# Differential attention: the rotary rows of a query or key tile are gathered by DMA and turned once a head

## The chip, the core and the metric

One core of a Trainium2 chip runs the whole program: two transformer blocks of two layers each, in one launch. The metric is the device time of one execution in microseconds. Three runs of the kernel before took 2494.85, 2496.67 and 2498.16 us; the median is 2496.67. The core has TensorE (matrix products and transposes through the identity), VectorE, ScalarE, GpSimd, and SyncE, which here only issues DMAs.

## The reference, cut to what matters

Sequence 512, model width 1024. The second layer of the first block is a differential attention with 8 heads. A head has two queries and two keys of 64 numbers and one value of 128. Of each 64 numbers only the first 16 are rotated by position, in pairs of number i and number i + 8:

```
q = _partial_rope(q, positions, 16, 500000.0)   # x1*cos - x2*sin , x2*cos + x1*sin on the first 16
k = _partial_rope(k, positions, 16, 500000.0)   # the other 48 of 64 pass unchanged
p1 = softmax(causal(q1 @ k1.T * 64 ** -0.5)); p2 = softmax(causal(q2 @ k2.T * 64 ** -0.5))
o = (p1 - lam * p2) @ v
o = rmsnorm(o, subln) * (1 - lambda_init)       # per head, then the output projection
```

The order of the 64 numbers within q and k may be changed in both alike, since only their dot products are used.

## The kernel before, in words

All products are taken in float32 quality as three float32r matmuls: an operand is split into a high part (a cast on ScalarE) and a low part (a subtraction, mostly on VectorE), by `split` (line 310), and `mm3` (line 345) adds high x high, high x low and low x high. Weights come in tiles of 128x1024 through SyncE: `dma_next` (line 134) loads one into one of two `raw` buffers, `split_next` (line 153) splits it into one of five `whi`/`wlo` pairs, and the next load waits until a `raw` buffer is free again.

The stage `diff` (line 970) holds everything of the attention. Activations lie transposed, numbers in partitions, 512 positions in columns. `fhead` (line 365) makes the query and key tiles of heads 0 and 1, half the columns at a time, while the layer norm before it finishes. `v_half` (line 958) makes the values in two halves. `projs(h)` (line 1027) is a generator which makes the query and then the key tile of a head, 24 matmuls each, in steps of 3. It gives control back after every step, and it waits at its gate until `self.unit`, the count of query tiles scored, is high enough. Every finished tile goes to `evac` (line 1004).

`evac` rotates all 128 rows by `rope` (line 652): a shuffle of the partitions out of PSUM on VectorE, a product with the cosine table, a product of the shuffled tile with the signed sine table, and an addition on GpSimd. The tables have 1 and 0 for rows that aren't rotated. Then it splits: a query's high part by a ScalarE cast, its low part on GpSimd, for each of the two halves of 64 rows; a key's high part twice by ScalarE casts and its low part on VectorE. After that `ready` holds the tile.

`attend` (line 623) walks over 8 heads and 4 query tiles. For a tile it emits `scores` (line 1034, eight matmuls in two PSUM banks, two softmaxes without normalising, and line 1054, which joins the two probability tiles), puts off the transposes of the joined tile by 6500 (`put`, key `sm`), and then lets `fill` (line 389) run a budget of other work from the queue `fq`, here the value half, the projections of heads 2 to 7, and the output projection. The budgets stand in `PLAN`: 30 for each of the first four tiles, then 11, and 9 for the last head. After a head's fourth tile come the value product `o`, sums of squares, and the scaling (`post`, line 1059).

Work that is put off stands in a list with due times (`defer`, line 321). The clock of that list counts TensorE columns as they are emitted (`tick`, line 328), and `need` (line 336) empties the list until something is ready. This gives the order of the program text. In `diff` only GpSimd keeps that order by hand (`hand=("Pool",)`). On TensorE, VectorE, ScalarE and SyncE a scheduler orders the instructions from its own estimate of when each is ready, earlier text first.

Of the kernel before, what the change touches and what calls it, by code (L numbers as in the profile page):

```python
# [9 lines left out]
F32 = mybir.dt.float32  # L10
F32R = mybir.dt.float32r
I32 = mybir.dt.int32
AF = mybir.ActivationFunctionType
ALU = mybir.AluOpType
# [3 lines left out]
D = 1024  # L18
S = 512
# [3 lines left out]
LAMBDA_INIT = 0.8 - 0.6 * math.exp(-0.3)  # L23
DFF1, DFF2 = 4096, 2816
MLA_SWAP = [i ^ 16 for i in range(32)]
DIFF_SWAP = [i ^ 8 if i < 16 else i for i in range(32)]
RING = 5
RAW = 2
AUTO = True
# [1 line left out]

PLAN = {
    "mla": dict(hand=("SP", "Pool"), ln=7000, sm=6000, pv=2500, eb=3, gate=5, cq=1500, n=([5] * 4 + [6] * 4) * 3 + [5] * 4 + [9] * 4),
    "diff": dict(hand=("Pool",), qp=1, kp=0, vp=1, wp=0, rp=0, nb=2, ln=7000, rot=3500, sm=6500, pv=2500, eb=3, sums=1000, scale=5500, n=[30] * 4 + [11] * 24 + [9] * 4),
    "fox": dict(ln=5500, sm=4200, pv=1500, eb=2, n=[30] * 4 + [11] * 24 + [9] * 4),
    "ret": dict(ln=5500, y=3900, n=30),
    "f0": dict(ln=7000), "f1": dict(ln=8500), "g0": dict(ln=5500), "g1": dict(ln=5500),
# [3 lines left out]
class Net:  # L41
# [620 lines left out]

    def rope_tables(self, pool, tmp, which, tags=("t0", "t1", "t2"), bufs=1):
        nc = self.nc
        C = pool.tile([128, S], F32, name="ropeC", bufs=1)
        Sn = pool.tile([128, S], F32, name="ropeS", bufs=1)
        pi = tmp.tile([128, S], I32, tag=tags[0], name="pi", bufs=bufs)
        a = tmp.tile([128, S], F32, tag=tags[1], name="ang", bufs=bufs)
        k = tmp.tile([128, S], F32, tag=tags[2], name="kk", bufs=bufs)
        inv = self.col[:, 2 * which:2 * which + 1]  # L670
        sgn = self.col[:, 2 * which + 1:2 * which + 2]
        (nc.gpsimd if which else nc.sync).dma_start(out=pi, in_=self.A["positions"].to_broadcast([128, S]))
        nc.vector.tensor_copy(a, pi)
        nc.vector.tensor_scalar(a, a, inv, None, op0=ALU.mult)
        MAG = 12582912.0
        nc.vector.tensor_scalar(k, a, 1.0 / (2 * math.pi), MAG, op0=ALU.mult, op1=ALU.add)
        nc.vector.tensor_scalar(k, k, -MAG, None, op0=ALU.add)
        c1 = 6.28125
        c2 = float(np.float32(2 * math.pi - c1).view(np.int32) & -4096)
        c2 = float(np.int32(np.float32(2 * math.pi - c1).view(np.int32) & -4096).view(np.float32))  # L680
        c3 = float(np.float32(2 * math.pi - c1 - c2))
        for cc in (c1, c2, c3):
            nc.vector.scalar_tensor_tensor(a, k, -cc, a, op0=ALU.mult, op1=ALU.add)
        PIF = 3.1415925
        nc.vector.tensor_scalar(a, a, PIF, -PIF, op0=ALU.min, op1=ALU.max)
        nc.scalar.activation(Sn, a, AF.Sin)
        nc.vector.scalar_tensor_tensor(a, a, -1.0, a, op0=ALU.mult, op1=ALU.min)
        nc.vector.tensor_scalar(a, a, math.pi / 2, None, op0=ALU.add)
        nc.scalar.activation(C, a, AF.Sin)
        nc.vector.tensor_scalar(Sn, Sn, sgn, None, op0=ALU.mult)  # L690
        return C, Sn

    def setup(self):
# [276 lines left out]
    def diff(self):  # L970
        nc, A, tc = self.nc, self.A, self.tc
        mm = nc.tensor.matmul
        with ExitStack() as outer:
# [27 lines left out]
            kls = [kz[:, 2 * i:2 * i + 2, :] for i in range(2)]  # L1001
            places = self.whole("c", F32)

            def evac(h, which):
                def f(ps):
                    r = self.rope(p, ps, DIFF_SWAP, C, Sn)


                    if which == 0:
                        qk[h] = [self.rs(n, F32R).rearrange("p (a n) -> p a n", a=2) for n in ("qa", "ka")]  # L1010
                        qk[h].append(kls[h % 2])
                    q, k, kl = qk[h]
                    for i in range(2):
                        own, other = slice(64 * i, 64 * i + 64), slice(64 - 64 * i, 128 - 64 * i)
                        if which == 0:
                            self.split(q[own, i, :], q[other, i, :], r[own], eng=nc.gpsimd if self.plan["qp"] else None)
                        else:
                            self.split(k[own, i, :], kl[own, i, :], r[own], eng=nc.gpsimd if self.plan["kp"] else None)
                            nc.scalar.copy(k[other, i, :], r[own])
                    ready.add((h, which))  # L1020
                return f

            self.fhead(4, lambda i, ps: evac(i // 2, i % 2)(ps))
            for _ in self.v_half(VH, VL, 0):
                pass

            def projs(h):
                for i in range(2):
                    while self.unit < 4 * h - 4 - (i == 0):
                        yield 0  # L1030
                    yield from self.proj(self.get, 0, 8, self.XH, self.XL, evac(h, i))
                self.need(lambda: (h, 1) in ready)

            def scores(h, qt):
                n, ts = qt * 128 + 128, slice(qt * 128, qt * 128 + 128)
# [23 lines left out]
            def post(h, o):  # L1059
                sq = places[:, 3, :]  # L1060
                nc.scalar.activation(sq, o, AF.Square)
                ot = p.tile([128, S], F32, tag="ot", name="ot", bufs=1)
                nc.scalar.copy(ot, o)
                rr = self.small(4, "rr")

                def sums():
                    sps = self.ps("sps")
                    for t in range(NT):
                        mm(sps[:, 2 * t:2 * t + 2], sq[:, t * 128:t * 128 + 128], ones, start=(t == 0), stop=(t == NT - 1))
                        self.tick(128, 4)  # L1070
                    s8 = self.small(8, "s8")
                    nc.vector.tensor_copy(s8, sps[:, 0:8])

                    nc.vector.tensor_tensor(rr, s1[h], s1[h], op=ALU.mult)
                    nc.vector.tensor_scalar(rr, rr, 1e-6, None, op0=ALU.mult)
                    nc.vector.scalar_tensor_tensor(rr, s8.rearrange("p (t a) -> p t a", a=2)[:, :, 0], 1.0 / 128, rr,
                                                   op0=ALU.mult, op1=ALU.add)
                    nc.gpsimd.tensor_tensor(rr, rr, self.mh, op=ALU.pow)
                    self.defer(self.plan["scale"], scale)

                def scale():
                    bp = self.ps("bp")
                    for t in range(NT):
                        self.transpose(bp[:, t * 128:t * 128 + 128], rr[:, t:t + 1].to_broadcast([128, 128]))
                    nc.vector.scalar_tensor_tensor(ot, ot, sub, bp, op0=ALU.mult, op1=ALU.mult)
                    self.split(VH[:, h, :], VL[:, h, :], ot, eng=nc.gpsimd if self.plan["vp"] else None)
                    nready[0] = h + 1

                self.defer(self.plan["sums"], sums)
# [334 lines left out]
ROPE_ORDER = np.array([16 * (i // 32) + i % 16 + 32 * (i % 32 // 16) for i in range(64)])  # L1424


def constants():
    c = {}
    c["c_idn"] = np.eye(128, dtype=np.float32)
    i = np.arange(128)  # L1430
    c["c_mask"] = np.zeros((128, S), np.float32)
    c["c_mask"][:, S - 128:] = np.where(i[None, :] <= i[:, None], 0.0, NEG)
    col = np.zeros((128, 16), np.float32)
    col[:, 0] = (10000.0 ** (-2.0 * (ROPE_ORDER[i % 64] % 32) / 64.0)).astype(np.float32)
    col[:, 1] = np.where(ROPE_ORDER[i % 64] < 32, -1.0, 1.0)
    d = i % 64
    col[:, 2] = np.where(d < 16, 500000.0 ** (-2.0 * (d % 8) / 16.0), 0.0).astype(np.float32)
    col[:, 3] = np.where(d < 8, -1.0, np.where(d < 16, 1.0, 0.0))
    c["c_col"] = col
    rows = np.zeros((32, 16), np.float32)  # L1440
    r = np.arange(32)
    kind = r // 8
    rows[:, 0] = kind == 0
    rows[:, 1] = kind == 1
    rows[:, 2] = kind >= 2
    rows[:, 3] = -1.0 * (kind == 2)
    rows[:, 4] = -1.0 * (kind == 3)
    rows[:, 5] = kind < 2
    rows[r, 8 + r % 8] = 1.0
    c["c_rows"] = rows  # L1450
    inv = (10000.0 ** (-np.arange(128) / 128.0)).astype(np.float32)
    ang = (np.arange(S, dtype=np.float32)[None, :] * inv[:, None]).astype(np.float32).astype(np.float64)
    c["c_rcos"] = np.cos(ang).astype(np.float32)
    c["c_rsin"] = np.sin(ang).astype(np.float32)
    key, q = np.arange(128)[:, None], np.arange(S)[None, :]
    dec = np.zeros((4, 128, S), np.float32)
    for h in range(4):
        gam = 1.0 - 2.0 ** (-5.0 - h)
        dec[h] = np.where(q // 64 >= key // 64, gam ** np.abs(q - key), 0.0)
    c["c_decay"] = dec  # L1460
    return c


def layout(I):
# [23 lines left out]
    for i in range(2):  # L1488
# [9 lines left out]
        n = DFF2 // 128  # L1498
# [3 lines left out]
        A[f"w_in{i}"] = gu.reshape(n // 2, 4, 128, D)[1:]  # L1502
        A[f"w_out{i}"] = pack_h(np.asarray(I["ffn_w_out_2"])[i])

    def heads(w):
        q, k = pack_f(w[:, :D]), pack_f(w[:, D:2 * D])
        v = np.concatenate([pack_v(np.ascontiguousarray(w[:, 2 * D + j * 512:2 * D + j * 512 + 512])) for j in range(2)])
        qk = np.stack([q, k], axis=1).reshape(16, 128, D)
        return np.concatenate([qk[:4], v, qk[4:]])

    A["w_d"] = heads(np.asarray(I["diff_w_qkv"])[0])
    A["w_do"] = pack_h(np.asarray(I["diff_w_o"])[0])
    wx = np.asarray(I["fox_w_in_2"])[0]
    A["w_x"] = heads(wx[:, :3 * D])
# [29 lines left out]
```

## Time and profile before

| | |
|---|---|
| median of the runs shown | 2496.67 us |
| the profiled execution | 2495.72 us |
| its span | 2492.5 us |
| TensorE busy | 2445.1 us (98%) |
| VectorE busy | 1644.9 us (66%) |
| ScalarE busy | 1113.9 us (45%) |
| GpSimd busy | 358.9 us (14%) |

The profile shows one execution. The span is the time from the first to the last instruction on record; the execution takes 3.2 us more. Busy shares are averages over eight stages with different limits. The granted TensorE clock was 0.997 of full speed over the span, which is the level of 2.4 GHz.

### The profile page before, as it was taken

How to read it: one execution, taken by the hardware profiler on the slowest of the kernel's cores; microseconds unless marked ns; L12 is line 12 of the kernel's file. 1: busy time of each engine (PE TensorE's matmuls, PEld its weight loads, DVE VectorE, ACT ScalarE, POOL GpSimd, SP SyncE). 2: the span in 40 equal slices, each digit the busy share in tenths (PEclk: the TensorE clock that was granted, in tenths of full speed). 3: DMA queues.
4: the chain of work that ended last, by engine and by line, in shares of the span. 5: the costliest groups of instructions: out<-in, count | busy, mean ns of one | idle time of the engine just before them, and what ended most of it. 6: DMA issues, size and time to landing. Idle time of an engine off the chain costs nothing.

```text
span 2492.5 us, 35902 instructions
## 1 busy us (share of the span) xinstructions
PE 2445.1 (98%) x14624; PEld 2176.4 (87%) x14624; DVE 1644.9 (66%) x2295; ACT 1113.9 (45%) x1664; POOL 358.9 (14%) x311
## 2 busy tenths in 40 slices
PE   9999999999989999999999999999999999999998
PEld 8889889888778988987888999988888888999987
DVE  6978758666987755755655877744454555877743
ACT  5635535424663543544454544533322233444532
POOL 2103002012342301104000222100000000222100
PEclk9999999999999999999999999999999999999999
DMA  4312332323121233232222333232322223233232
GB/s 151 109 68 94 97 126 87 102 79 102 52 90 61 88 103 129 82 102 87 85 68 77 102 102 104 90 100 83 124 79 86 81 85 107 81 118 111 77 104 73
DMA packets 65860, 233.40 MB, mean 94 GB/s; under 512 B 7536, under 2 KB 7680, under 8 KB 65696
## 3 DMA queue, kind: packets, MB, share of 16 engines
q1 hardware_dynamic: 62064, 219.21, 26.9%
q0 software_dynamic: 3488, 11.55, 1.4%
q8 instruction: 114, 1.87, 0.3%
q10 hardware_dynamic: 144, 0.36, 0.1%
q14 instruction: 50, 0.41, 0.1%
HBM read 228.99 MB, written 2.10 MB: 93 GB/s over the span
## 4 chain that ended last, share of the span: by engine, by line
PE 52%; POOL 1%; DVE 0%; ACT 0%; issue 0%; DVEq 0%; POOLq 0%; ACTq 0%
PE zA L266 3%; PE zA L267 3%; PE zA L268 3%; PE ta L349 2%; PE ta L347 2%; PE ta L348 2%; PE tb L349 2%; PE tb L348 2%; PE tb L347 2%; PE ps L347 2%; PE ps L349 2%; PE ps L348 2%; PE pj L347 2%; PE pj L349 2%; PE pj L348 2%; PE v L347 2%
## 5 line engine op out<-in xcount | busy, mean ns | idle before, releaser
L313 ACT CAST whi<-raw 128x1024 fp32r<-128x1024 f32 (+3 forms) x347 | 359.5, 1038 | 592.3 <-PE ta L349 143.0
L314 DVE TENSOR_TENSOR wlo<-raw,whi 128x1024 fp32r<-128x1024 f32 (+3 forms) x347 | 430.3, 1243 | 281.8 <-ACT whi L313 281.5
L314 DVE TENSOR_TENSOR wlo<-qt,whi 128x1024 fp32r<-128x1024 f32 x102 | 168.0, 1647 | 33.5 <-ACT whi L313 33.5
L347 PE MATMUL ps<-XH,whi 128*128 128x256 f32 (+1 forms) x576 | 177.9, 309 | 0.0
L348 PE MATMUL ps<-XL,whi 128*128 128x256 f32 (+1 forms) x576 | 176.7, 307 | 0.0
L349 PE MATMUL ps<-XH,wlo 128*128 128x256 f32 (+1 forms) x576 | 176.7, 307 | 0.0
L267 PE MATMUL zB<-XL,whi 128*128 128x256 f32 x544 | 154.1, 283 | 0.3 <-DVE XL L314 0.3
L268 PE MATMUL zB<-XH,wlo 128*128 128x256 f32 x544 | 153.9, 283 | 0.0
L266 PE MATMUL zB<-XH,whi 128*128 128x256 f32 x544 | 153.9, 283 | 0.0
L313 ACT CAST whi<-qt 128x1024 fp32r<-128x1024 f32 x102 | 107.1, 1050 | 96.8 <-PE zA L267 75.8
L196 POOL TENSOR_TENSOR qt<-raw,qt 128x1024 f32<-128x1024 f32 x34 | 98.1, 2885 | 307.4 <-DVE wlo L314 251.0
L196 POOL TENSOR_TENSOR qt<-qr,raw 128x1024 f32<-128x1024 f32 x34 | 85.4, 2512 | 339.7 <-PE ta L348 182.3
L347 PE MATMUL pj<-XH,whi 128*128 128x512 f32 x288 | 116.7, 405 | 0.0
L349 PEld LDWEIGHTS ps<-XH,wlo 128*128 128x128 f32 x576 | 109.8, 191 | 5.1
L348 PEld LDWEIGHTS ps<-XL,whi 128*128 128x128 f32 x576 | 109.9, 191 | 5.0
L347 PEld LDWEIGHTS ps<-XH,whi 128*128 128x128 f32 x576 | 109.9, 191 | 5.0
L349 PE MATMUL pj<-XH,wlo 128*128 128x512 f32 x288 | 113.0, 392 | 0.0
L348 PE MATMUL pj<-XL,whi 128*128 128x512 f32 x288 | 112.5, 390 | 0.0
L267 PEld LDWEIGHTS zB<-XL,whi 128*128 128x128 f32 x544 | 104.4, 192 | 0.5 <-DVE XL L314 0.5
L314 DVE TENSOR_TENSOR wlo<-qr,whi 128x1024 fp32r<-128x1024 f32 x68 | 83.3, 1226 | 31.9 <-ACT whi L313 31.8
L268 PEld LDWEIGHTS zB<-XH,wlo 128*128 128x128 f32 x544 | 104.4, 192 | 0.0
L266 PEld LDWEIGHTS zB<-XH,whi 128*128 128x128 f32 x544 | 104.4, 192 | 0.0
(480 smaller groups left out, 7462.9 us busy)
## 6 DMA issues: line engine op xcount, KB each, us to landing
raw<-in_w_r SPq DMA_DIRECT2D x48, 512.0 KB, 3.5
raw<-in_w_out SPq DMA_DIRECT2D x44, 512.0 KB, 3.4
qr<-in_w_in SPq DMA_DIRECT2D x40, 512.0 KB, 4.4
raw<-in_w_in SPq DMA_DIRECT2D x40, 512.0 KB, 3.5
raw<-in_w_d SPq DMA_DIRECT2D x24, 512.0 KB, 3.5
raw<-in_w_x SPq DMA_DIRECT2D x24, 512.0 KB, 3.4
raw<-in_w_dn0a SPq DMA_DIRECT2D x16, 512.0 KB, 3.5
raw<-in_w_dn0b SPq DMA_DIRECT2D x16, 512.0 KB, 3.4
```

The costliest lines, as they stand in the source:

```text
L196: eng.tensor_tensor(t, a, b, op=ALU.subtract)
L266: mm(out, a, sh[:, k, :], start=f, stop=False, skip_group_check=True)
L267: mm(out, a, sl[:, k, :], start=False, stop=False, skip_group_check=True)
L268: mm(out, b, sh[:, k, :], start=False, stop=e, skip_group_check=True)
L313: nc.scalar.copy(hi, src)
L314: (eng or nc.vector).tensor_tensor(lo, src, hi.bitcast(F32), op=ALU.subtract)
L347: mm(ps, ah, bh, start=first, stop=False)
L348: mm(ps, ah, bl, start=False, stop=False)
L349: mm(ps, al, bh, start=False, stop=last)
```

## The change

Query and key weights are packed with a new order of columns (`DIFF_ORDER`), so that the rotated numbers of both halves of a tile lie in rows 48 to 79, the two of a pair side by side. A finished tile is copied whole out of PSUM to `rq` by ScalarE. Three DMAs on SyncE's queue gather its 32 rows: straight into `rot`, and with the two of each pair exchanged into rows 64 and up of `swp`. When both tiles of a head are there, `turn` does three VectorE operations on 64 rows and two DMAs put the rows back into `rq`. `parts` does the splits that `evac` did before, and only it makes the head `ready`. `turn` is put off by 3000 after the key tile's copy, `parts` by another 5000. At the head of the stage, the tiles of head 1 are held in PSUM until `parts(0)` has run.

The tables share one tile, cosine in rows 0 to 63, signed sine in rows 64 to 127. In `post` the scaling by `sub` moves into the ScalarE copy. The budget of the 24 middle tiles is 12 in place of 11, the gate of `projs` is one query tile lower for both tiles of a head, and its `need` at the end is gone.

```
-    "diff": dict(..., rot=3500, sm=6500, ..., n=[30] * 4 + [11] * 24 + [9] * 4),
+    "diff": dict(..., rot=3000, back=5000, sm=6500, ..., n=[30] * 4 + [12] * 24 + [9] * 4),
@@ rope_tables
-        C = pool.tile([128, S], F32, name="ropeC", bufs=1)
-        Sn = pool.tile([128, S], F32, name="ropeS", bufs=1)
+        C = Sn = pool.tile([128, S], F32, name="ropeC", bufs=1)
+        if not which:
+            Sn = pool.tile([128, S], F32, name="ropeS", bufs=1)
+        lo, hi = (slice(64, 128), slice(0, 64)) if which else (slice(0, 128),) * 2
...
@@ diff
+            got = {}
             def evac(h, which):
                 def f(ps):
-                    r = self.rope(p, ps, DIFF_SWAP, C, Sn)
+                    if which == 0:
+                        got[h] = [[], p.tile([128, S], F32, tag="rot", name="rot", bufs=1),
+                                  p.tile([128, S], F32, tag="swp", name="swp", bufs=1)]
+                    rs, rot, swp = got[h]
+                    r = p.tile([128, S], F32, tag="rq", name="rq", bufs=2)
+                    rs.append(r)
+                    nc.scalar.copy(r, ps)
+                    o = 32 * which
+                    nc.sync.dma_start(out=rot[o:o + 32], in_=r[48:80])
+                    nc.sync.dma_start(out=swp[64 + o:96 + o:2], in_=r[49:80:2])
+                    nc.sync.dma_start(out=swp[65 + o:96 + o:2], in_=r[48:80:2])
+                    if which == 1:
+                        self.defer(self.plan["rot"], lambda: turn(h))
+                return f
+
+            def turn(h):
+                rs, rot, swp = got[h]
+                a, b = rot[0:64], swp[0:64]
+                nc.vector.tensor_tensor(a, a, C[0:64], op=ALU.mult)
+                nc.vector.tensor_tensor(b, swp[64:128], Sn[64:128], op=ALU.mult)
+                nc.vector.tensor_tensor(a, a, b, op=ALU.add)
+                for w in range(2):
+                    nc.sync.dma_start(out=rs[w][48:80], in_=rot[32 * w:32 * w + 32])
+                self.defer(self.plan["back"], lambda: parts(h))
+
+            def parts(h):
+                for which, r in enumerate(got.pop(h)[0]):
                     if which == 0:
...
                     ready.add((h, which))
-                return f
-            self.fhead(4, lambda i, ps: evac(i // 2, i % 2)(ps))
+                for which, ps in enumerate(held):
+                    evac(1, which)(ps)
+                held.clear()
+            held = []
+            self.fhead(4, lambda i, ps: held.append(ps) if i > 1 else evac(0, i)(ps))
...
             def projs(h):
                 for i in range(2):
-                    while self.unit < 4 * h - 4 - (i == 0):
+                    while self.unit < 4 * h - 6 + i:
                         yield 0
                     yield from self.proj(self.get, 0, 8, self.XH, self.XL, evac(h, i))
-                self.need(lambda: (h, 1) in ready)
@@ post
-                nc.scalar.copy(ot, o)
+                nc.scalar.activation(ot, o, AF.Copy, scale=sub)
...
-                    nc.vector.scalar_tensor_tensor(ot, ot, sub, bp, op0=ALU.mult, op1=ALU.mult)
+                    nc.vector.tensor_tensor(ot, ot, bp, op=ALU.mult)
@@ packing
+_turn = np.arange(16) // 2 + np.arange(16) % 2 * 8
+DIFF_ORDER = np.concatenate([np.arange(16, 64), _turn, 64 + _turn, np.arange(80, 128)])
```

## Rows read from the trace of the kernel before

**Rows 1.** waits of TensorE, 500 to 840: us in all, times, longest

```profile
PE pt L353 <- DVE xc L1054: 8.9, 7, 1.6
...
PE o L348 <- DVE xb L314: 2.1, 5, 0.9
PE o L347 <- ACT xa L313: 1.7, 4, 0.7
PE v L347 <- DVE VL L314: 1.4, 1, 1.4
```

**Rows 2.** TensorE in order of time: start us, us, operation, operands

```profile
666.26 0.39 PE L349 MATMUL pj<-XH,wlo 128*128 128x512 f32 x1
...
669.11 0.60 PE L1043 MATMUL s<-ka,qa 128*128 128x384 f32 x2
...
676.86 0.39 PE L347 MATMUL pj<-XH,whi 128*128 128x512 f32 x1
...
677.09 0.39 PE L348 MATMUL pj<-XL,whi 128*128 128x512 f32 x1
...
678.98 0.52 PE L353 MATMUL pt<-idn,xc 128*128 128x128 f32 x3 [1.50 <-DVE xc L1054]
...
679.25 0.48 PE L349 MATMUL pj<-XH,wlo 128*128 128x512 f32 x1
...
679.92 0.42 PE L1043 MATMUL s<-ka,qa 128*128 128x128 f32 x2
```

**Rows 3.** stretches: length, busy us of PE, PEld, DVE, ACT, POOL, clock, DMA

```profile
540.00:575.00 35.00, 35.00 (x254) 33.17 (x253) 25.01 (x44) 13.56 (x19) 14.70 (x13) 1.00 0.33 96
...
659.12:679.92 20.80, 18.84 (x105) 15.61 (x104) 18.96 (x51) 14.11 (x32) 8.73 (x6) 1.00 0.17 52
```

**Rows 4.** VectorE, and one GpSimd instruction, in order of time

```profile
668.44 0.73 DVE L656 STREAM_SHUFFLE rt<-pj 128x512 f32<-128x512 f32 x1
...
670.79 1.45 POOL L659 TENSOR_TENSOR rt<-rt,rt 128x512 f32<-128x512 f32 x1 [2.78 <-DVE rt L658]
...
671.03 2.29 DVE L314 TENSOR_TENSOR wlo<-raw,whi 128x1024 fp32r<-128x1024 f32 x1
...
673.45 0.54 DVE L592 CUSTOM_DVE_ANT_0 xc<-s,mask 128x384 f32<-128x384 f32 x1
...
678.22 0.61 DVE L1054 SCALAR_TENSOR_TENSOR xc<-e,r,xc 128x384 f32<-128x384 f32 x1
```

**Rows 5.** groups of instructions, 540 to 830: count | busy us, mean ns | idle before

```profile
L656 DVE STREAM_SHUFFLE rt<-pj 128x512 f32<-128x512 f32 x12 | 8.9, 738 | 0.0
...
L657 DVE TENSOR_TENSOR rt<-pj,ropeC 128x512 f32<-128x512 f32 x12 | 8.1, 678 | 0.0
...
L658 DVE TENSOR_TENSOR rt<-rt,ropeS 128x512 f32<-128x512 f32 x16 | 13.0, 813 | 0.0
...
L659 POOL TENSOR_TENSOR rt<-rt,rt 128x512 f32<-128x512 f32 x16 | 27.3, 1705 | 76.1 <-DVE rt L658 75.9
...
L314 DVE TENSOR_TENSOR xd<-rt,ka 64x512 fp32r<-64x512 f32 x16 | 11.0, 686 | 7.5 <-ACT ka L313 7.1
...
L1063 ACT COPY ot<-o 128x512 f32<-128x512 f32 x8 | 4.6, 580 | 0.0
...
L313 ACT CAST qa<-rt 64x512 fp32r<-64x512 f32 x16 | 9.9, 620 | 10.9 <-POOL rt L659 10.7
```

**Rows 6.** low parts of weights on VectorE, 540 to 760: ns min/median/max

```profile
L314 DVE TENSOR_TENSOR wlo<-raw,whi x30: 1214/1224/2308, 540.6 to 750.0; 128x1024 fp32r<-128x1024 f32 x30
```

**Rows 7.** DMA issues by tile: count, KB each, median us to landing

```profile
out<-nt SPq DMA_DIRECT2D x8, 256.0 KB, 2.0
...
raw<-in_w_d SPq DMA_DIRECT2D x24, 512.0 KB, 3.5
...
few<-in_diff_subln POOLq DMA_DIRECT2D x1, 0.5 KB, 5.6
```

**Rows 8.** waits of SyncE's DMA queue, 593 to 760

```profile
SPq L149 <- DVE wlo L314: 108.1, 12, 14.0
```

More of the change, by code (lines that the diff above doesn't have):

```diff
@@ L25 @@
 MLA_SWAP = [i ^ 16 for i in range(32)]
-DIFF_SWAP = [i ^ 8 if i < 16 else i for i in range(32)]
 RING = 5
@@ L33 @@
     "mla": dict(hand=("SP", "Pool"), ln=7000, sm=6000, pv=2500, eb=3, gate=5, cq=1500, n=([5] * 4 + [6] * 4) * 3 + [5] * 4 + [9] * 4),
-    "diff": dict(hand=("Pool",), qp=1, kp=0, vp=1, wp=0, rp=0, nb=2, ln=7000, rot=3500, sm=6500, pv=2500, eb=3, sums=1000, scale=5500, n=[30] * 4 + [11] * 24 + [9] * 4),
+    "diff": dict(hand=("Pool",), qp=1, kp=0, vp=1, wp=0, rp=0, nb=2, ln=7000, rot=3000, back=5000, sm=6500, pv=2500, eb=3, sums=1000, scale=5500, n=[30] * 4 + [12] * 24 + [9] * 4),
     "fox": dict(ln=5500, sm=4200, pv=1500, eb=2, n=[30] * 4 + [11] * 24 + [9] * 4),
@@ L685, in rope_tables @@
         nc.vector.tensor_scalar(a, a, PIF, -PIF, op0=ALU.min, op1=ALU.max)
-        nc.scalar.activation(Sn, a, AF.Sin)
+        nc.scalar.activation(Sn[lo], a[lo], AF.Sin)
         nc.vector.scalar_tensor_tensor(a, a, -1.0, a, op0=ALU.mult, op1=ALU.min)
         nc.vector.tensor_scalar(a, a, math.pi / 2, None, op0=ALU.add)
-        nc.scalar.activation(C, a, AF.Sin)
-        nc.vector.tensor_scalar(Sn, Sn, sgn, None, op0=ALU.mult)
+        nc.scalar.activation(C[hi], a[hi], AF.Sin)
+        nc.vector.tensor_scalar(Sn[lo], Sn[lo], sgn[lo], None, op0=ALU.mult)
         return C, Sn
@@ L1435, in constants @@
     col[:, 1] = np.where(ROPE_ORDER[i % 64] < 32, -1.0, 1.0)
-    d = i % 64
-    col[:, 2] = np.where(d < 16, 500000.0 ** (-2.0 * (d % 8) / 16.0), 0.0).astype(np.float32)
-    col[:, 3] = np.where(d < 8, -1.0, np.where(d < 16, 1.0, 0.0))
+    col[:, 2] = (500000.0 ** (-2.0 * (i % 16 // 2) / 16.0)).astype(np.float32)
+    col[:, 3] = np.where(i % 2, 1.0, -1.0)
     c["c_col"] = col
@@ L1503, in layout, with heads @@
         A[f"w_out{i}"] = pack_h(np.asarray(I["ffn_w_out_2"])[i])
-    def heads(w):
+    def heads(w, order=None):
+        if order is not None:
+            w = w[:, np.concatenate([np.tile(order, 16) + 128 * (np.arange(2048) // 128), np.arange(2 * D, 3 * D)])]
         q, k = pack_f(w[:, :D]), pack_f(w[:, D:2 * D])
@@ L1509, in heads @@
         return np.concatenate([qk[:4], v, qk[4:]])
-    A["w_d"] = heads(np.asarray(I["diff_w_qkv"])[0])
+    A["w_d"] = heads(np.asarray(I["diff_w_qkv"])[0], DIFF_ORDER)
     A["w_do"] = pack_h(np.asarray(I["diff_w_o"])[0])
```

## The prediction

> **What bounds the kernel now.** The share of busy time says TensorE, everywhere, so the first view to read is what TensorE waits for, over the only stage that the change touches in its work, the differential attention (about 540 to 770 us). Four kinds of wait make nearly all of it [rows 1]: the probability transposes `pt` wait 8.9 us in all for line 1054 on VectorE, the value products `o` 2.1 us for VectorE's low part and 1.7 us for ScalarE's cast, and 1.4 us go once on a `v` bank. These 14.1 us are all that this change can give back unless it shortens TensorE's own work, and no matmul of it is touched.
>
> Next, the order of TensorE around the longest of these waits [rows 2]. The last matmul of a key projection (666.26) stands ahead of the third query tile's scores (669.11). The transposes of that tile come at 678.98, after a wait of 1.50 us, and the next head's first scores at 679.92. The transpose sits between the second and third matmul of one projection step, where the program text never puts it: the order on TensorE, and on ScalarE, VectorE and SyncE, is the scheduler's, made from what it expects to be ready. The wait is then what the chip does later than expected. It comes seven times [rows 1], once before each of the last heads: six waits of 1.0 to 1.6 us and, in the tail, one of 0.2, so 8.7 of the 8.9 repeat.
>
> Why it is late is seen on VectorE. In one head of 20.80 us it is busy 18.96, more than TensorE's 18.84 [rows 3]. Between 668.44 and 678.83 [rows 4] it works off the shuffle, the products with the tables, a weight's low part of 2.29 us, and only at 673.45 reaches the mask of the scores begun at 669.11 [rows 2].
>
> **The change, part by part.** Profiled execution: 2495.72 us, span 2492.5; the median of the runs shown is 2496.67, so 0.95 is added at the end.
>
> *Off VectorE and GpSimd.* Per projected tile VectorE loses a shuffle (0.738), a product from PSUM (0.678) and a product with the sine (0.813), and GpSimd an addition (1.705) [rows 5]. Per head (two tiles) that is 4.46 us of VectorE and 3.4 of GpSimd. VectorE gains three operations on 64 rows per head: the row of the same shape, 64x512, has 0.686, no less than the 128-row ones, so 2.06. Net 2.4 us a head. On top, the low part of a weight takes 1.22 in the median and 2.31 at most [rows 6]; the one of 671.03 met the rotary addition that began on GpSimd at 670.79 [rows 4]. Without that addition it is 1.1 shorter. For the interval of rows 4: out go 0.74 + 0.68 + 0.69 of rotation, two 0.69 for the key's low parts (they move behind the rotation) and the 1.1, together 4.6; in come at most 2.06. The queue ahead of line 1054 gets 2.5 us shorter, the wait is 1.5. **Term a: -8.7 us**, the six repeated waits; bounds 0 and -8.9.
>
> *The waits at `o`.* ScalarE's casts of the query, which stood before the cast of the last probabilities, move to another place, and VectorE is shorter. But the six casts now come in one burst. I take somewhat less than half of the 3.8 us [rows 1]: **term b: -1.5**; bounds 0 and -3.8. The single 1.4 us on `v` I leave where it is (bounds 0 and -1.4): the weights there, not the rotation, set VectorE's pace.
>
> *On ScalarE.* One 128x512 copy from PSUM per tile, 0.580 [rows 5], 1.16 a head; it was busy 14.11 of 20.80 [rows 3], so it has room in the sum. The scaled copy in `post` replaces an unscaled one of equal shape, and a two-input product replaces a three-input operation in `scale`: 0.07 us of VectorE a head, hidden. The tables are made of half as many rows; since 64 rows cost what 128 do, nothing. The four tiles at the head of the stage have TensorE full beside them (35.00 of 35.00 us [rows 3]) and the value half still ahead of the first scores, 16 steps of 6 matmuls at 0.23, 22 us; so their new path costs nothing. Were that cover gone, one chain of 14 us as below would stand open.
>
> *The added chain.* This is the cost. From the end of the key projection to the next head's first scores there are now: copy on ScalarE 0.58 with half a microsecond of queue (1.1); three gathers on the weight queue; three VectorE operations, 2.06 with half a microsecond of queue (2.6); two transfers back; six casts on ScalarE of 0.62 (3.7); the last low part on VectorE (0.7). No small transfer within the core stands in the trace. The nearest by kind are the store of 256 KB on this queue, 2.0 us to landing, and the weight loads of 512 KB, 3.5; the slowest, on another queue, is 5.6 [rows 7]. I take 2.5, near the store, since 64 KB is less than either but a weight load may be under way, and 0.3 for each further issue: 3.2 and 2.8. Sum 14.1. What there is: from 666.65 to 679.92 less the wait that goes, 11.8 us. The chain is 2.3 late. Behind it TensorE has the next key projection, which needs none of it: 12 matmuls at 0.23 (676.86 to 677.09 [rows 2]) are 2.8 us for the first half, 5.5 for both. The scheduler can set these ahead, as it did with `pt`. What stays is what the chip does later than expected, and the nearest row is the wait at `o`, also a TensorE step behind a ScalarE cast and a VectorE low part: 2.1 us over 5 times and 1.7 over 4, 0.4 each [rows 1]. I take a little more, 0.5, for each of seven heads: **term c: +3.5**; bounds 0 and, with 5.6 us for both trips (chain 20.3, late 8.5, less 5.5), 3.0 each or +21.
>
> The page SBUF — State Buffer of the Trainium skill (The DMA setup-cost knee) gives every transfer a fixed cost of about 2 us, mostly until the write is confirmed, plus the bytes over 436 GB/s: an estimate of 2.15 us for 64 KB. By it the chain would be 0.7 shorter and still 1.6 late, and term c the same. It speaks against a change that puts two such trips in a row for 64 KB. Its sizes fit the rows only roughly: it makes the store 2.6 where 2.0 is measured and the weight load 3.2 where 3.5 is; no run so far shows the small copy itself.
>
> *The projections "sooner".* I price this at nothing, because it does not change the order. A projection yields in steps of 3. A budget of 11 lets four steps run (3, 6, 9, 12), and so does 12. The first four query tiles, with 30 each, take the 16 value steps of 6 (96) and the query projection of head 2 (24): exactly 120. After that each head uses 48 in four tiles, so head h's query projection starts at tile 4h-5, where the old gate already opens, and the new, earlier gate finds the queue still busy with the head before. Rows 2 show that place: the key ends one tile before the third scores. The dropped `need` was always met already.
>
> Sum: -8.7 - 1.5 + 3.5 = -6.7; 2489.0 for the profiled execution, **2490.0** as a median.
>
> **The rivals.**
> *A, the wait moves.* The chain is late and the order doesn't cover it: each head's first scores wait 1.3 us or so. For it: 2.3 us late by my own sum, and the casts in one burst between the exponentials. Against it: 2.8 us of matmuls at hand. 7 x 1.3 = 9.1 against 10.2 gained: 2495.6.
>
> *B, slower: the weight queue's order.* SyncE stands before a weight load until VectorE has freed its buffer: 108.1 us over 12 loads here, 9.0 each, the longest 14.0 [rows 8]. Transfers behind such a load wait with it. With 9.0 more the chain is 23.1, late by 11.3, and after 5.5 of cover 5.8 stand open. In three of seven heads, the others as forecast: 17.4 + 2.0 - 10.2 = +9.2, 2505.9; in all seven 2527. It decides from about 4.7 us of queueing a head on, where the loss (1.5 a head) eats the gain. Against it: the load becomes ready only after the freed weight's cast and low part, about 2.3 us of work that starts with the same event as the 0.58 copy, so the gather should be queued first.
>
> *C, all waits go*, with no new one: 2496.67 - 14.1 = 2482.6. For it: VectorE has 3 us a head to spare afterwards. Against: a chain longer than its gap.
>
> *D, the projections do come sooner* against my count: the chain gains a query tile, some 5 us, term c is 0: 2486.5.
>
> **How the numbers follow.** Forecast 0.52, own range 2486 to 2494; A 0.25; B 0.13; C 0.07; D 0.03. A measurement of this kernel tells about 0.2%, 5 us, from no change: faster means below 2491.7, slower above 2501.7. Of the forecast about a quarter (0.13) lies above 2491.7. Faster 0.39 + 0.07 + 0.03 and a little of A: 0.50. Same 0.13 and most of A and a little of B: 0.37. Slower, B: 0.13. The range from 2483 to 2501 leaves out some of C and nearly all of B.
>
> **What would show it.** Right: `pt` waits for line 1054 fall from 8.9 to under 2 us; VectorE near 16 us a head; the head's first scores behind 12 or more matmuls of the next key projection, with waits of about 0.5 us; gathers landing in 2 to 3 us; the projections in the same places between the scores. Wrong: waits of a microsecond or more at the first scores (A), gathers issued long after their copy (B), TensorE waiting on ScalarE casts elsewhere, or a period that stays near 20.7 us a head.

## The result and the profile after

The changed kernel takes 2521.4 us (2518.6 to 2524.4, 4 runs) against 2497.4 for four runs of the kernel before made beside it: 1.0097 times as long, interval 1.0081 to 1.0113. It is 24 us slower. The forecast was 2490.0, with a range of 2483 to 2501: the time is outside the range, and on the other side of the time before. The profiled execution took 2518.63 us.

The whole loss lies in the differential attention. From its first `ps` matmul to the first transpose (`tp`) of the output projection's result it took 245.5 us before and takes 269.4 now, 23.9 more. The next two rows are this stage as a stretch, of the kernel before:

```profile
540.60:786.10 245.50, 229.87 (x1242) 193.47 (x1242) 193.78 (x455) 130.79 (x276) 78.37 (x61) 1.00 0.25 78
```

and of the kernel after (columns as in [rows 3]: length, busy us of TensorE, its weight loads, VectorE, ScalarE, GpSimd, then the granted clock):

```profile
541.10:810.50 269.40, 242.35 (x1243) 204.20 (x1242) 176.09 (x415) 139.66 (x292) 57.02 (x45) 0.94 0.28 83
```

VectorE lost 17.7 us and GpSimd 21.4, as meant. TensorE has the same matmuls (1243 on record, 1242 before), yet it is busy 12.5 us longer, at a mean clock of 0.94, and idle 27.1 us where it was 15.6. So the loss has two halves: 11.4 us more waiting and 12.5 us of the same work done more slowly. Both rows are of one profiled execution each.

Waits of TensorE after, 540 to 830 us (us in all, times, longest); they answer to [rows 1]:

```profile
PE s L1077 <- POOL qa L313: 15.6, 9, 3.4
PE s L1077 <- ACT ka L1051: 7.5, 2, 5.1
...
PE o L346 <- ACT xa L312: 0.7, 1, 0.7
PE s L1079 <- DVE xd L313: 0.6, 3, 0.2
PE pt L352 <- DVE xc L1088: 0.2, 1, 0.2
```

All that the change was to remove is gone: `pt` from 8.9 to 0.2, `o` from 3.8 to 0.7, the wait on `v` altogether. In their place stand 23.7 us at the scores (L1077 and L1079, the lines 1043 and 1045 of before), for the query's low part, which GpSimd makes, and for the key's casts on ScalarE. They fall on heads 2 to 7, with 7.5, 2.8, 4.4, 4.4, 4.1 and 0.6 us; head 1 waits for nothing.

Head 2, whose 7.5 us are the waits for casts, has one cause of its own. On ScalarE the copy of the next query tile (642.39) stands between the second and third of the key's four casts. It waits 1.24 us for GpSimd's low part, which still reads one of the two `rq` buffers, and the last two casts wait behind it.

TensorE in order of time around the first scores of one head; it answers to [rows 2]:

```profile
677.89 0.39 PE L348 MATMUL pj<-XH,wlo 128*128 128x512 f32 x1
...
680.03 0.60 PE L1077 MATMUL s<-ka,qa 128*128 128x384 f32 x2
...
688.62 0.60 PE L352 MATMUL bp<-idn,rr 128*128 128x128 f32 x4
692.63 0.33 PE L1077 MATMUL s<-ka,qa 128*128 128x128 f32 x1 [3.41 <-POOL qa L313]
693.18 0.33 PE L1079 MATMUL s<-xd,qa 128*128 128x128 f32 x1 [0.22 <-DVE xd L313]
694.31 0.44 PE L1077 MATMUL s<-ka,qa 128*128 128x128 f32 x1 [0.80 <-POOL qa L313]
...
695.14 0.73 PE L346 MATMUL pj<-XH,whi 128*128 128x512 f32 x1
...
699.18 0.40 PE L1077 MATMUL s<-ka,qa 128*128 128x256 f32 x2
```

Three things are to be seen here. The key projection still ends (677.89) right before the third tile's scores (680.03), as in [rows 2]. The first scores (692.63) wait 3.41 us and then twice more. And the 12 matmuls of the next projection, which need nothing of the chain, stand behind these scores (695.14 to 699.18), not ahead. They take 4.0 us there, where 12 at 0.23 take 2.8.

The chain that these scores wait for, on ScalarE, SyncE, VectorE and GpSimd in turn (start, us, operation):

```profile
678.09 1.05 ACT L312 CAST whi<-raw 128x1024 fp32r<-128x1024 f32 x1 [1.06 <-PE pj L347]
679.05 0.58 ACT L1018 COPY rq<-pj 128x512 f32<-128x512 f32 x1
...
688.59 1.04 ACT L312 CAST whi<-raw 128x1024 fp32r<-128x1024 f32 x1
689.54 1.25 ACT L312 CAST qa<-rq 64x512 fp32r<-64x512 f32 x2
...
679.65 0.51 SPq L1020 DMA_DIRECT2D rot<-rq  x1
...
686.02 1.14 SPq L1034 DMA_DIRECT2D rq<-rot  x2
...
682.65 0.68 DVE L1030 TENSOR_TENSOR rot<-rot,ropeC 64x512 f32<-64x512 f32 x1
...
685.28 0.68 DVE L1032 TENSOR_TENSOR rot<-rot,swp 64x512 f32<-64x512 f32 x1
...
691.47 3.34 DVE L313 TENSOR_TENSOR xd<-rq,ka 64x512 fp32r<-64x512 f32 x2
...
690.28 3.97 POOL L313 TENSOR_TENSOR qa<-rq,qa 64x512 fp32r<-64x512 f32 x2 [4.70 <-ACT qa L312]
```

The granted clock (third number from the end) around the first scores of heads 3 and 4, which are at 666.49 (after 2.05 us of waiting, and 0.76 more at 668.05) and at 692.63; the last row is the same stretch of head 5:

```profile
669.00:674.40 5.40, 5.40 (x17) 4.43 (x17) 3.59 (x7) 2.08 (x6) 1.47 (x1) 0.55 0.36 98
674.40:679.00 4.60, 4.60 (x26) 3.93 (x25) 2.24 (x8) 2.48 (x6) 0.00 (x0) 1.00 0.07 29
695.00:699.20 4.20, 4.20 (x14) 3.37 (x15) 1.17 (x7) 0.99 (x4) 1.49 (x2) 0.67 0.49 152
699.20:704.00 4.80, 4.80 (x27) 4.19 (x26) 2.35 (x9) 2.76 (x7) 0.00 (x0) 1.00 0.02 7
...
719.90:724.00 4.10, 4.10 (x11) 3.23 (x11) 1.03 (x5) 0.98 (x4) 1.31 (x2) 0.50 0.52 158
```

TensorE is busy for the whole of 669.0 to 674.4, and most of that runs at the lower level, 1.2 GHz: up to 673.6 its 512-column matmuls follow one another every 0.43 us, and every 0.23 us from 674 on. The same is seen behind the first scores of heads 2 (0.50 over 5.2 us from 644.8) and 6 (0.62 over 4.2 us from 745.8), not behind head 7's. In the kernel before, the pause of 1.50 us at 678.98 [rows 2] has nothing of the kind behind it:

```profile
677.40:679.00 1.60, 0.10 (x2) 0.06 (x1) 1.43 (x5) 1.28 (x4) 0.26 (x1) 1.00 0.00 0
679.00:683.00 4.00, 4.00 (x24) 3.48 (x25) 3.75 (x9) 2.08 (x5) 1.23 (x1) 1.00 0.02 6
```

Groups after, 540 to 830 us (count | busy us, mean ns | idle before); they answer to [rows 5]:

```profile
L313 POOL TENSOR_TENSOR qa<-rq,qa 64x512 fp32r<-64x512 f32 x16 | 27.0, 1685 | 54.3 <-ACT qa L312 53.7
L313 DVE TENSOR_TENSOR xd<-rq,ka 64x512 fp32r<-64x512 f32 x16 | 19.5, 1218 | 9.5 <-ACT ka L312 9.3
...
L1018 ACT COPY rq<-pj 128x512 f32<-128x512 f32 x12 | 7.0, 581 | 2.5 <-POOL qa L313 2.5
```

The small transfers (count, KB each, median us to landing), beside [rows 7]:

```profile
rot<-rq SPq DMA_DIRECT2D x16, 64.0 KB, 1.9
swp<-rq SPq DMA_DIRECT2D x32, 32.0 KB, 1.8
rq<-rot SPq DMA_DIRECT2D x16, 64.0 KB, 1.9
```

And what SyncE's queue waited for, 593 to 785 us, beside [rows 8]:

```profile
SPq L1020 <- ACT rq L1018: 65.7, 11, 10.5
SPq L148 <- DVE wlo L313: 39.1, 8, 7.6
```

### The profile page after: what moved, and what is told of

Read it like the earlier page. It is cut to its first block, busy times and chain, and to the rows that moved or that the text cites. A ratio compares the mean times of both kernels' runs of the same rounds, so it can differ in the third digit from the quotient of the medians.

```text
span 2516.8 us, 36023 instructions
## 1 busy us (share of the span) xinstructions
PE 2457.8 (98%) x14624; PEld 2187.5 (87%) x14624; DVE 1630.7 (65%) x2255; ACT 1121.9 (45%) x1680; POOL 336.9 (13%) x295
## 4 chain that ended last, share of the span: by engine, by line
PE 51%; DVE 1%; issue 1%; POOL 1%; ACT 0%; DMA 0%; DVEq 0%; POOLq 0%; ACTq 0%
PE zA L265 3%; PE zA L267 3%; PE zA L266 3%; PE ta L348 2%; PE ta L347 2%; PE ta L346 2%; PE tb L348 2%; PE tb L346 2%; PE tb L347 2%; PE ps L346 2%; PE ps L348 2%; PE ps L347 2%; PE pj L346 2%; PE pj L348 2%; PE pj L347 2%; PE v L346 2%
## 5 line engine op out<-in xcount | busy, mean ns | idle before, releaser
L313 DVE TENSOR_TENSOR wlo<-raw,whi 128x1024 fp32r<-128x1024 f32 (+3 forms) x347 | 423.8, 1224 | 292.3 <-ACT whi L312 291.7
```

What stands on the lines that cost most here:

```text
L313: (eng or nc.vector).tensor_tensor(lo, src, hi.bitcast(F32), op=ALU.subtract)
```

## The experiments

Theory: the first scores stand where the chain ends, nothing covers the rest of it, and the clock falls behind the pause. Rivals: the gathers queue behind weight loads; the budget and the gate do the harm; GpSimd's part is the slow link; the waits alone, without the clock, are the loss. Diffs are against the kernel after, unless they say otherwise. The table gives the stage as the two rows above do: its length, TensorE's idle and busy time in it, from one profiled execution, and beside it the median device time. The ratio is to runs of the kernel before made beside each experiment, whose medians were 2495.2 to 2497.4 us, so that differences between the device times of two rows are good to some 2 us.

| kernel | stage us | idle | busy | device us | ratio to before |
|---|---|---|---|---|---|
| before | 245.5 | 15.6 | 229.9 | 2497.4 | |
| after | 269.4 | 27.1 | 242.4 | 2521.4 | 1.0097 |
| 1 no transfers | 235.6 | 6.9 | 228.7 | 2484.7 | 0.9945 [0.9930, 0.9960] |
| 2 projections earlier | 246.3 | 12.7 | 233.6 | 2496.7 | 0.9997 [0.9987, 1.0006] |
| 3 query low parts on VectorE | 263.9 | 21.8 | 242.1 | 2511.8 | 1.0058 [1.0036, 1.0079] |
| 4 16 unread matmuls | 264.6 | 11.5 | 253.2 | 2517.5 | 1.0077 [1.0062, 1.0092] |
| 5 cover by text order | 244.3 | 10.9 | 233.4 | 2494.6 | 0.9994 [0.9984, 1.0003] |
| 6 before, budgets of 2 | 258.5 | 19.7 | 238.8 | 2507.9 | 1.0048 [1.0033, 1.0063] |
| 7 projections one tile earlier | 245.2 | 11.4 | 233.8 | 2495.0 | 0.9995 [0.9986, 1.0005] |
| 8 = 7 and 3 | 239.0 | 9.2 | 229.8 | 2488.9 | 0.9976 [0.9965, 0.9987] |
| 9 = 5 and 3 | 235.9 | 5.4 | 230.5 | 2486.6 | 0.9962 [0.9948, 0.9976] |
| 10 10 unread matmuls | 268.7 | 16.9 | 251.8 | 2517.9 | 1.0088 [1.0072, 1.0103] |
| 11 no gathers | 246.3 | 12.9 | 233.4 | 2496.2 | 1.0002 [0.9993, 1.0012] |
| 12 before, order of 5 | 256.9 | 19.9 | 237.0 | 2506.2 | 1.0042 [1.0025, 1.0059] |

**1. No transfers.** The turn works on the copied tiles.

```
-  three gathers per tile, two returns per head
+  turn: rs[0][0:64], rs[1][64:128] in place
```

> Leaves out the five transfers of a head; the three VectorE operations work in place on rows of the copied tiles, so the rotation isn't computed. Theory (the chain copy, gather, turn, back, splits is longer than the gap before the next head's scores): without about 3.0 us of gather and 2.5 us of return the splits end some 5.5 us sooner, the waits of 2.1 to 5.1 us at the first scores of heads 2 to 6 go below 0.5, the granted clock stays at 1.00 in every stretch from 600 to 760, and the time is 2485 to 2493, below the kernel before. Rival 1 (the burst of six casts and two GpSimd low parts is late by itself): half of the waits stay, 2505 to 2515. Rival 2 (something outside the chain, as ScalarE's added copies): within 5 us of the changed kernel's 2521.

Measured 2484.7, just under the range: 36.7 us under the kernel after and 12 under the kernel before. The waits at the scores fall from 23.7 to 4.0 us (540 to 830 us):

```profile
PE s L1070 <- POOL qa L313: 4.0, 3, 2.4
```

The theory wanted less than that: head 2 still waits 2.36 and 0.90 us, and the clock behind is 0.62 over 4.5 us. The relief of VectorE is real, and the transfers eat it three times over.

**2. Projections two tiles earlier in fact.** The budgets are raised so that the queue is empty when a gate opens.

```
-  n=[30]*4 + [12]*24 + [9]*4            gate 4*h - 6 + i
+  n=[36]*4 + [12]*20 + [6]*4 + [9]*4    gate 4*h - 8 + i
```

> The projections truly two query tiles sooner: budget 36 in place of 30 for the first four tiles, 6 for tiles 25 to 28, gate two tiles lower; the rotation as in the changed kernel. Theory (lateness of one chain of some 16 us against a gap of 12): two tiles more, some 10 us, cover it whole; no wait at the first scores, clock 1.00, 2484 to 2494, below the kernel before. Rival (the burst or the transfers disturb other work wherever they stand): waits appear elsewhere, 2500 or more.

Measured 2496.7, between the theory's range and the rival's. The waits at the scores go, but `pt` waits 4.0 us again and `sps` (the sums of squares) 3.3 for ScalarE, as the rival has it: the burst of casts and low parts probably falls among the other steps now. The clock falls here too, behind a wait of 1.22 us ahead of the sums of squares (694.87):

```profile
694.90:699.30 4.40, 4.40 (x20) 3.69 (x21) 1.52 (x3) 3.68 (x7) 1.33 (x2) 0.71 0.40 134
```

**3. Query low parts on VectorE.**

```
-  qp=1
+  qp=0
```

> Only the query's low parts go from GpSimd to VectorE (qp=0). In the changed kernel these two on GpSimd take 3.97 us together and end the wait. Theory (the last link is GpSimd, slowed by the key's low parts on VectorE): the wait at the first scores falls by about 2.5 us a head, the slow stretch after it shortens, 2500 to 2510. Rival (the transfers alone decide, the low parts hide behind the six casts on ScalarE): under 0.7 us a head, 2515 to 2522.

Measured 2511.8, just above the range; 9.6 us better. The rows of the same two groups in this kernel:

```profile
L313 DVE TENSOR_TENSOR xd<-rq,ka 64x512 fp32r<-64x512 f32 x16 | 11.0, 687 | 1.6 <-ACT ka L312 1.3
L313 DVE TENSOR_TENSOR qa<-rq,qa 64x512 fp32r<-64x512 f32 x16 | 11.0, 686 | 2.9 <-ACT qa L312 2.4
```

A key's low part takes 0.69 us again, where it took 1.22 in the mean beside GpSimd. All four low parts of a head are 2.7 us on VectorE; they were 3.97 on GpSimd with 3.34 beside it on VectorE. GpSimd was one link of the chain, not the cause: 18 us of waits at the scores stay.

**4. 16 unread matmuls** ahead of the first scores of heads 2 to 7.

```
+  d = self.ps("dm")
+  for i in range(16):
+      mm(d, self.XH[:, i % 8, 0:128], self.XH[:, 0, :], ...)
```

> Adds 16 matmuls of 512 columns (some 3.7 us at full clock) whose product nobody reads, directly before the first scores of heads 2 to 7, where TensorE now waits 2.1 to 5.1 us. Theory (the pause also costs the clock: 12 matmuls after it take 4.0 to 5.2 us where they took 2.8): the same late scores, but the clock stays at 1.00 from 640 to 760, and the time falls by 6 to 14 us, to 2507 to 2515, although TensorE does more. Rival (the slow stretch has another cause, or the added matmuls only push the scores back): 2521 to 2540.

Measured 2517.5, above the theory's range and under the rival's. Row of this stage:

```profile
543.40:808.00 264.60, 253.15 (x1339) 214.89 (x1338) 176.05 (x414) 139.47 (x292) 57.37 (x45) 0.99 0.28 85
```

The clock is back at 0.99 (head 2 alone, with waits of 1.39 and 2.65 us, still has 0.50 behind it). A set of 16 takes 3.8 us, so 22.6 of the 253.2 busy us are the added work; the rest, 230.6, is that of before (229.9). The slower clock is thus a real 12 us. But the filler fills a place that work must fill, and is no work: 15.6 us of waits and 11.8 of clock come back, 22.6 are spent, net 4.8 of the stage.

**5. The cover, by the text order.**

```
+  swap = "back" in self.plan and h > 1 and qt == 0
+  if swap: self.fill(...)        # a projection's 12 matmuls
   e = scores(h, qt)
   ...
-  self.fill(...)
+  if not swap: self.fill(...)
```

> From head 2 on, the 12 matmuls of the next key projection stand in the text before a head's first scores and not behind them; nothing else changes. This is the cover that the prediction counted on and that the scheduler didn't give. Theory (the first scores come 3 to 5 us too early for the chain, and the pause then halves the clock): 2.8 us of matmuls fill most of the pause, waits at the first scores fall to 0 to 1.5 us a head, the clock stays at 1.00, the time falls by 15 to 27 us to 2494 to 2506. Rival (the scores of two tiles in a row then delay their exponentials, and the transposes wait instead): waits at the probability transposes of 1 us and more, 2508 or more.

Measured 2494.6, 26.8 us under the kernel after (25.7 by the two ratios), with nothing left out and nothing but the place of one budget of work a head changed. The matmuls now stand ahead of a head's first scores (head 4 here), and 7.7 us of idle time are left at the scores, 3.9 of them for the key's low part:

```profile
699.52 0.39 PE L348 MATMUL pj<-XH,wlo 128*128 128x512 f32 x1
699.75 0.22 PE L1081 MATMUL s<-ka,qa 128*128 128x128 f32 x1
700.19 0.33 PE L1081 MATMUL s<-ka,qa 128*128 128x128 f32 x1 [0.22 <-POOL qa L313]
```

```profile
PE s L1083 <- DVE xd L313: 3.9, 6, 1.6
```

This is the step that the prediction took as given. The clock does not stay at 1.00 everywhere, as the theory had it: behind the first scores of heads 2 and 5 it is 0.62 and 0.63 over 4.5 us.

**6. The kernel before with the budgets and gates of 2.**

> The kernel before, its rotation untouched, with the budgets (36, 12, 6, 9) and gates of the run with two tiles of lead. It tells what the budgets alone do. If they are neutral: within 4 us of the kernel before, so that the run with lead (2496.7) has gained nothing from the new rotation because its splits stall other work. If taking 24 steps' columns from tiles 25 to 28 costs: 2500 to 2510, and the new rotation with enough lead is worth the difference.

Measured 2507.9: with the old rotation the same lead costs 12 us. So in 2 the new rotation is worth 11 us (13 by the ratios), and the other budgets and gates take as much.

**7 and 8. One tile earlier; the same with 3.**

```
-  n=[30]*4 + [12]*24 + [9]*4
+  n=[30]*3 + [42] + [12]*21 + [6, 6, 12] + [9]*4
```

> The changed kernel with the projections one query tile sooner (budget 42 in tile 4, 6 in tiles 26 and 27; gates as changed). One tile is about 5 us; the chain was 3.4 to 5 us late at its first half and 0.8 us more at its second. Theory: waits at the first scores under 0.5 us, clock 1.00, 2486 to 2497. Rival (as in the run with two tiles, the burst of six casts then delays the exponentials or the squares): waits of 1 us and more at the transposes or the sums of squares in most heads, 2495 to 2503.

> As the run before with one tile of lead, and the query's low parts on VectorE in place of GpSimd. VectorE has had room (27 to 30 us of 40), and the two engines no longer slow each other in the splits. Theory: as with one tile, and 1 to 4 us less, 2484 to 2494. Rival (VectorE's order is what delays the transposes): more than with one tile alone.

Measured 2495.0 and 2488.9; both times lie in the theory's ranges. In 7 the mechanism is not as the theory had it: 5.8 us of waiting stay at the scores, up to 1.3 us each where under 0.5 was expected, 2.9 us go at `o`, and the clock is 0.71, 0.66 and 0.58 over 4 to 5 us behind the first scores of heads 2, 3 and 5. In 8 the time is 6.1 us less than in 7, where 1 to 4 were expected. With GpSimd out of the chain, one tile of lead is nearly enough: 2.7 us of waiting stay at the scores, 3.7 at `pt`, and the stage's clock is 1.00.

**9. 5 and 3 together.**

> The kernel after with the next key's 12 matmuls in front of a head's first scores in the text (from head 2) and the query's low parts on VectorE. Theory (a head's first scores stand where the chain of 15 to 16 us ends, with 2.8 us of cover, and the GpSimd low parts of 2 us each are its slowest link): the waits at the first scores of 3.9 + 2.4 + 1.1 us seen with the cover alone fall to under 4, no pause reaches 2 us, the clock stays at 1.00, and the time is 2487 to 2493, some 4 us under the 2494.6 of the cover alone. Rival (VectorE takes 2.8 us a head more, and the probability transposes wait for line 1054 as they did before): 2494 to 2499, with 4 us or more of waits at pt.

Measured 2486.6, a little under the range: faster than the kernel before by 0.38% and than the changed one by 1.4%, with the clock at 1.00 from 640 to 760. Its longest waits from 540 to 800 us:

```profile
PE o L346 <- ACT xa L312: 1.4, 2, 0.7
PE ta L348 <- POOL VL L313: 1.0, 2, 0.6
PE s L1081 <- ACT ka L1055: 1.0, 3, 0.4
```

**10. 10 unread matmuls in place of 16.**

> The kernel after with 10 matmuls of a tile that nothing reads in front of each head's first scores (heads 2 to 7), where an earlier run had 16. They take 2.3 us at full clock and delay nothing that is needed, as the scores come some 3.4 to 5 us late. Theory (a pause of 3 us and more halves the clock afterwards, and that costs more than the pause): pauses fall to 1 to 2.5 us, the clock stays near 1.00, and the time is 2505 to 2513, under both the 2521.4 without and the 2517.5 with 16. Rival (the clock is a small part, the loss is the wait itself): 2516 to 2523.

Measured 2517.9: the theory's number missed, and the time lies in the rival's range. I expected the clock near 1.00 once the pauses were under 2.5 us. They are, at 1.1 and 0.8 us in heads 4 to 6, and the clock falls all the same:

```profile
689.88 0.33 PE L1081 MATMUL s<-ka,qa 128*128 128x128 f32 x1 [1.12 <-POOL qa L313]
...
691.55 0.33 PE L1081 MATMUL s<-ka,qa 128*128 128x128 f32 x1 [0.80 <-POOL qa L313]
```

(the key's low part adds 0.22 and 0.23 us behind each), and the stretch right behind them:

```profile
692.00:697.00 5.00, 4.90 (x16) 3.95 (x17) 1.38 (x8) 1.00 (x5) 1.74 (x2) 0.66 0.44 131
```

Four waits with a short matmul between each did what one wait of 1.50 us in [rows 2] did not. Less 14.1 us of filler, 237.7 us of busy time stay, 7.8 above before: the rival's time, but not its reason. That a pause of 3 us is needed was already contradicted by head 3 of the kernel after, where the clock fell behind 2.05 and 0.76 us.

**11. No gathers;** the turn works on the copied tiles, the two returns stay.

> Leaves out the three gathers of each tile: the turn works on the copied tiles in place, and the two transfers back stay (the values of the rotated rows are not the reference's). Theory (every microsecond of the chain stands open at the first scores, and a pause under 2 us leaves the clock alone): the gathers' issues and landing, about 3.6 us of the chain of 14.5, go; the first scores wait 0 to 1.5 us a head, and the time is 2492 to 2503, so that the gathers cost 18 to 29 us of the 36.7 that all five transfers cost. Rival (the transfers back, next to the burst of casts and low parts, are the link that decides): 2508 to 2518, with waits of 2 us and more at the first scores.

Measured 2496.2, in the theory's range. Taken out first, the three gathers give back 25 of the 36.7 us, and the two returns after them 11.5 (24 and 14 by the ratios): every link of the chain counts. The theory's word on the clock did not hold: behind waits of 1.61 and 0.80 us at head 3's first scores it is 0.68 over 4.5 us.

**12. The kernel before with the order of 5.**

> The kernel before with only the order in the text changed: from head 2 on, the budget of a head's first query tile (12 matmuls of the next projection) stands in front of that tile's scores. Theory (the place of these matmuls pays only where the first scores come late, and with the old rotation they do not; its waits are at the transposes behind line 1054, whose queue on VectorE stays as long): 2494 to 2501, with some 6 us or more still waited at pt. Rival (the place itself is worth something with either rotation, since VectorE gets 2.8 us more for the join before TensorE needs it, so that the best version owes its gain to the order and not to the new rotation): 2486 to 2491, with pt under 3 us.

Measured 2506.2, worse than the theory's 2494 to 2501 and far from the rival's 2486 to 2491. TensorE's waits from 540 to 830 us:

```profile
PE pt L353 <- DVE xc L1058: 7.4, 6, 2.2
PE o L347 <- ACT xa L313: 7.1, 5, 2.4
```

The waits at `o` have grown, from 3.8 to 9.4 us with those for VectorE, and the clock falls in this kernel too: behind the wait of 2.20 us at 679.52 it is 0.66 over 5 us. So the order helps only the new rotation, and version 9 owes its gain to both. Whether the kernel before would gain from its query low parts on VectorE, the third part of version 9, was not run.

## Why the prediction was wrong

**The step that failed** is the one on the chain: "The scheduler can set these ahead, as it did with `pt`. What stays is what the chip does later than expected". The scheduler did not. The 12 matmuls stand behind the first scores, and the whole lateness stands open: 23.7 us at the scores where term c had 3.5. Experiment 5 puts these matmuls ahead by the text and is back at 2494.6, so this step carries the loss. The gain that was forecast does not come with it: 5 is as fast as the kernel before, not faster. That the scheduler had pulled one transpose into a projection step was no evidence that it would pull a projection over scores. Why it did not is open: in its own estimate the chain may be shorter than on the chip. That the next query tile's copy has to wait for one of the two `rq` buffers is less likely to be the reason: in experiment 5 the 12 matmuls end (699.52) before that copy starts (700.32).

**A second cost was not in the sum at all.** A wait was priced at its own length, in the forecast and in every rival. Here the clock reads 0.50 to 0.67 for some 4 to 5 us behind the first scores of heads 2 to 6, and that is worth 12.5 us more. The rows of before could not show it, since the clock stays at 1.00 behind their single pauses. The Trainium skill has it: in TensorE: Matmul & The Clock Gate, HAM oscillation — how this bites in real kernels, waits between groups of matmuls throw the engine to its lower level in every round of a loop. The trace agrees, in five of the six heads that wait (the 0.50 to 0.67 above). It would have been a rival with a price of its own.

**The chain's length** was nearly right. Estimated 14.1 us from the key projection's end; measured from 678.1 to the first half's scores at 692.63, 14.5, and to the second's 16.2. By links: copy with its queue 1.5 (estimate 1.1: a weight's cast of 1.05 stood ahead of it), gathers 3.0 (3.2; the sum's own terms, 2.5 and twice 0.3, give 3.1), turn 3.3 (2.6: other VectorE work in between), returns and the next weight cast 3.6 (2.8), casts and low parts to the first scores 3.1 (4.4, but for both halves). What the estimate left out is GpSimd: the query's low parts stayed there, start behind the first cast (690.28), and take 2.30 and 1.60 us beside VectorE's, so that they end (694.25) after the last cast (693.36). The gap was estimated at 11.8 us; TensorE's other work ended at 689.2, 11.1 after the chain's start.

That VectorE and GpSimd slow each other bears on a rule of SBUF — State Buffer in the Trainium skill (SBUF: two separate sides): the two engines share one pair of ports, and between a GpSimd operation that reads this memory and a VectorE operation with both inputs in it, as here, whichever starts first keeps the pair for its whole instruction. The trace agrees: two of each ran from 690.28 to 694.81, and a key's low part took 1.66 us in place of 0.69.

**Right:** term a (-8.7 forecast, 8.9 to 0.2 measured). Term b was low: -3.1 in place of -1.5, and the wait on `v` went too (-1.4). The "sooner" projections, at nothing: the key's end stands where it stood, and with the old budget and gate in the new kernel the order of instructions is the same on every engine. The transfers land in 1.9 and 1.8 us where 2.5 was taken. The costs at the stage's head were nothing: the second head's first scores are at 618.19, and were at 619.51.

**The rivals:** A had the place (the order doesn't cover) but 1.3 us a head in place of 3.4 on average, since it used the same chain without GpSimd, and no clock. (Both A and term c count seven heads; heads 2 to 7, six, wait, 4.0 us each on average.) B, which held the slower side, did not happen: the gather of 679.65 is issued as the copy ends (679.05 + 0.58), and it is now the queue that waits for the copy, 65.7 us, while its waits on `wlo` fell from 108.1 to 39.1. C's time, 2482.6, is near what 1 and 9 reach (2484.7 and 2486.6), with the transfers left out or covered.

## What to carry to other kernels

When a change trades engine work for latency, name the instructions that cover the latency and where the text puts them; a scheduler's order elsewhere is no promise, and an explicit order is cheap. Price a TensorE wait that comes back every round as the wait and the slower work behind it; here that doubled it. And when work leaves a busy engine, look at what is left on the slow one (GpSimd here): a link that was hidden before becomes the last one.

## What the runs showed of the hardware

- The granted clock fell after 3.41, 0.22 and 0.80 us of waiting (0.67 over 4.2 us), and also after 1.12, 0.22, 0.80 and 0.23 us with one short matmul between each (0.66 over 5 us), but not after single waits of 1.50 (before) and 1.34 us (experiment 4) between full streams.
- The length of a wait alone did not settle it: behind one wait of 2.20 us the clock was 0.66 over 5 us (experiment 12, 679.52), behind another it stayed at 1.00 (experiment 2, 643.10), and behind one of 1.22 us with a few two-column matmuls after it (experiment 2, 694.87) it was 0.71 over 4.4 us.
- Transfers within the core of 32 and 64 KB on SyncE's queue land in 1.8 and 1.9 us, and each issue takes the queue 0.5 to 0.6 us. A chain with two such trips spent 6.6 of 14.5 us on them, a weight's cast behind the second included.
- VectorE's 64x512 subtraction took 0.69 us alone and up to 1.66 beside GpSimd's.
